# One five-bank score tile for the attention, and the second scan's products in the attention's ring

## The chip, the cores and the metric

The kernel runs on one core of one Trainium2 chip. The metric is the device time of one execution in microseconds (us); the kernel before took 2292.06 us, the median of three runs (2285.45 to 2292.4). Lower is better. TensorE (PE) multiplies matrices, VectorE (DVE) and ScalarE (ACT) work on vectors and read the matmul results out of PSUM, GpSimd (POOL) works on SBUF alone, SyncE (SP) issues the DMAs. PSUM has eight banks here, each 128 partitions by 512 float32 columns. "Granted clock" is the share of its full 2.4 GHz that TensorE ran at.

## The reference

Two layers run over 1280 tokens (256 of context, then 1024 latent ones). In each, one normalised input goes through one input projection into three parallel branches whose outputs are joined by one output projection:

```python
def hybrid_layer(x_l, x_c, mod_l, mod_c, ...):
    h_l = rmsnorm(x_l) * (1 + scale_l) + shift_l          # the same for the context
    p_l = split_cols(h_l @ w_in, IN_SPLITS)
    gdn_c, gdn_l = gdn_branch(...)    # gated DeltaNet: 4 heads, chunks of 64, a scan both ways
    mla_c, mla_l = mla_branch(...)    # 8 heads of softmax attention
    gla_c, gla_l = gla_branch(...)    # gated linear attention: 4 heads, a scan both ways
    x_l = x_l + gate_l * (jnp.concatenate([gdn_l, mla_l, gla_l], axis=-1) @ w_out)

def attend(q, k, v):
    s = jnp.einsum('bqhd,bkhd->bhqk', q, k).astype(jnp.float32) * MLA_SCALE
    p = jax.nn.softmax(s, axis=-1).astype(v.dtype)
    return jnp.einsum('bhqk,bkhd->bqhd', p, v)
```

Latent queries attend to all 1280 keys, context queries to the 256 context keys. In the last layer the context's outputs are not needed and are left out.

## The kernel before, in words

A layer runs in stages (`run`, L1432): the input projection and the preparation of the scans, `up` (the attention's query, key and value projections), `attend` (L1147), `proj_start` (L1309: it loads and transposes the branches' outputs, splits the first weights of the output projection and makes the gates), and `proj`. Beside `up` and `attend` a *background* generator is drawn forward, one step at each `yield` of the attention: the DeltaNet scan `gdn_scan` (20 steps; its first product on TensorE is `kS`, L743), `gla_prep`, eight levels `gla_level` of GLA (score products `gsc`, L887 and L906, then copies into `A`, then new operands `qx` and `kc`, L937, and the decays, L919), and `gla_scan` (10 steps: a transpose `kdt`, outputs `gO`, the state's update `gF`). What of it is left after `attend` is drained there.

The attention's unit is 128 queries of one head: 64 units in layer 1, and in layer 0 the same 64 and eight context units of two tiles each. For a wide unit `first` forms 1024 score columns (tile `sa`: 2 buffers of two banks) and their row maximum (L1219); `second` forms the last 256 (`sb`, half a bank for each of two units), their maximum (L1238), joins both (L1239), and takes two exponentials into `P` (L1240, L1241), each with its row sum. A product by split halves (`mm3`, L254) is three matmuls (L256 to L258). `transposed` turns `P` in groups of 4, 4 and 2 blocks (`ptr`, L1256) and copies them to `PT` (L1260: ACT, DVE, ACT). After each four units `output` multiplies by the values (`O`, L1268).

PSUM in this stage: `sa` 4 banks, `sb` 1, ring "t" 2 (`ptr` and `O` take turns in it), "l" 1 (all that the background's GLA and `proj_start` put in PSUM). Program order is the order of emission in Python, in which the background's last step comes within the first dozen or so units. A scheduler then fixes a static order on each engine, and every engine works through its own in that order; buffers of one ring are still given out in the order of emission.

Of the kernel before, what the change touches and what calls it, by code (L numbers as in the profile page):

```python
# [9 lines left out]
F32 = mybir.dt.float32  # L10
F32R = mybir.dt.float32r
U32 = mybir.dt.uint32
AF = mybir.ActivationFunctionType
ALU = mybir.AluOpType
AX = mybir.AxisListType
# [4 lines left out]
T = 1280  # L20
CT = 2
# [23 lines left out]
class Net:  # L45
# [893 lines left out]
    def gla_scan(self, l):  # L939
        nc, sp = self.nc, self.sp  # L940
        last = l == L - 1
        mm = nc.tensor.matmul
        V, A, P = nc.vector, nc.scalar, nc.gpsimd
        Q, K, tot = (self.lst[n] for n in ("Q", "K", "tots"))

        def at(i):

            return self.A5[i // 2][:, 512 * (i % 2):512 * (i % 2) + 512]

        oL = [self.bp.tile([128, 512], F32, name="oL", tag="oL", bufs=5) for _ in range(5)]  # L950
        order = (tuple(range(10)), (1, 0) + tuple(range(9, 1, -1)))
        S = [None, None]
        for st in range(10):
            vs, kt = [], None
            for d in range(2):
                vv = sp.tile([128, 256], F32, name="gvt", tag="gvt", bufs=4)
                nc.sync.dma_start(vv, self.gv_d[l][order[d][st]])
                vs.append(vv)
            if st < 9:
                pk = self.g("kdt", "l")  # L960
                for d in range(2):
                    i = order[d][st]
                    nc.tensor.transpose(pk[:, 128 * d:128 * d + 128], K[d][:, 128 * i:128 * i + 128], self.ident)
                kt = sp.tile([128, 256], F32, name="ktl", tag="ktl", bufs=2)
                A.copy(kt, pk[:, 0:256])
                yield
            todo = [d for d in range(2) if not (last and order[d][st] < CT) and (d == 0 or S[d] is not None)]
            if todo:
                ps = self.g("gO", "l")
                for d in todo:  # L970
                    i = order[d][st]
                    pd = ps[:, 256 * d:256 * d + 256]
                    if S[d] is not None:
                        mm(pd, Q[d][:, 128 * i:128 * i + 128], S[d], start=True, stop=(d == 1))
                    if d == 0:
                        for hd in range(4):
                            mm(pd[:, 64 * hd:64 * hd + 64], at(i)[:, 128 * hd:128 * hd + 128], vs[0][:, 64 * hd:64 * hd + 64],
                               start=(S[d] is None), stop=(S[d] is None or hd == 3))
                for d in todo:
                    i = order[d][st]  # L980
                    o = oL[i // 2][:, 256 * (i % 2):256 * (i % 2) + 256]
                    pd = ps[:, 256 * d:256 * d + 256]

                    other = (1 - i if i < 2 else 11 - i) if d == 0 else i
                    if st < other or (d == 0 and i == 1):
                        A.copy(o, pd)
                    else:
                        V.tensor_tensor(o, pd, o, ALU.add)
                yield
            if st < 9:  # L990
                pf = self.g("gF", "l")
                for d in range(2):
                    mm(pf[:, 256 * d:256 * d + 256], kt[:, 128 * d:128 * d + 128], vs[d], start=True, stop=True)
                Sn = sp.tile([128, 512], F32, name="Sl", tag="Sl", bufs=2)
                V.tensor_tensor(Sn.rearrange("p (d n) -> p d n", d=2), pf.rearrange("p (d n) -> p d n", d=2),
                                self.bdm.unsqueeze(1).broadcast_to([128, 2, 256]), ALU.mult)
                for d in range(2):
                    Sd = Sn[:, 256 * d:256 * d + 256]
                    if S[d] is not None:
                        i = order[d][st]  # L1000
                        V.scalar_tensor_tensor(Sd, S[d], tot[:, d, i:i + 1], Sd, ALU.mult, ALU.add)
                    S[d] = Sd
            for j in {1: (0,), 7: (2, 3), 9: (1, 4)}.get(st, ()):
                self.head_norm(l, 1, oL[j], j)
            yield
# [141 lines left out]
    def attend(self, l, fill=None):  # L1147
        nc, sp = self.nc, self.ap
# [34 lines left out]

        groups = [(m, i) for m in range(4) for i in range(lt0, NT, 2)]
        units = [(m, i + j, hh) for m, i in groups for hh in range(2) for j in range(1 if i < CT else 2)]
        sb, mxs, sas, ps, PT, rds = {}, {}, {}, {}, {}, {}

        def scores(u, dst, c0, cn, j=0):
            m, i, hh = units[u]
            q, k = [t[:, hh] for t in qTs[m, i - i % 2][0:2]], kTs[m][hh]  # L1190
            J = slice(128 * (i % 2 + j), 128 * (i % 2 + j) + 128)
            self.mm3(dst, q[0][:, J], q[1][:, J], k[0][:, c0:c0 + cn], k[1][:, c0:c0 + cn], True, True)
# [7 lines left out]
                if (m, i - i % 2) not in qTs:  # L1200
                    load_q(m, i - i % 2)

        def first(u, c0):

            m, i, hh = units[u]
            if i < CT:
                if c0 == 0:
                    sas[u] = sa = self.ps.tile([128, 1024], F32, name="sa", tag="sa", bufs=2)[:, 0:512]
                    for j in range(2):
                        scores(u, sa[:, 256 * j:256 * j + 256], 0, 256, j)  # L1210
                    mxs[u] = mx = sp.tile([128, 2], F32, name="mx", tag="mx", bufs=4)
                    V.tensor_reduce(mx, sa.rearrange("p (j k) -> p j k", j=2), AX.X, ALU.max, negate=True)
                return
            if c0 == 0:
                sas[u] = self.ps.tile([128, 1024], F32, name="sa", tag="sa", bufs=2)
            scores(u, sas[u][:, c0:c0 + 512], c0, 512)
            if c0 == 512:
                mxs[u] = mx = sp.tile([128, 2], F32, name="mx", tag="mx", bufs=4)
                V.tensor_reduce(mx[:, 0:1], sas[u], AX.X, ALU.max, negate=True)  # L1219

        def second(u):

            m, i, hh = units[u]
            mx, ta = mxs.pop(u), sas.pop(u)
            if hh == 0 and i % 2 == 0:
                rds[m, i] = sp.tile([128, 2, 2, 2], F32, name="rd", tag="rd", bufs=3)
            r = rds[m, i - i % 2][:, hh, i % 2, :]
            ps[u] = p = self.ab.tile([128, T], F32, name="P", tag="P", bufs=PB)
            if i < CT:
                for j in range(2):  # L1230
                    J = slice(256 * j, 256 * j + 256)
                    A.activation(p[:, J], ta[:, J], AF.Exp, bias=mx[:, j:j + 1], accum_out=r[:, j:j + 1])
                return
            if u // 2 not in sb:
                sb[u // 2] = self.ps.tile([128, 512], F32, name="sb", tag="sb", bufs=1)
            tb = sb[u // 2][:, 256 * (u % 2):256 * (u % 2) + 256]
            scores(u, tb, 1024, 256)
            V.tensor_reduce(mx[:, 1:2], tb, AX.X, ALU.max, negate=True)  # L1238
            V.tensor_tensor(mx[:, 0:1], mx[:, 0:1], mx[:, 1:2], ALU.min)  # L1239
            A.activation(p[:, 1024:T], tb, AF.Exp, bias=mx[:, 0:1], accum_out=r[:, 1:2])  # L1240
            A.activation(p[:, 0:1024], ta, AF.Exp, bias=mx[:, 0:1], accum_out=r[:, 0:1])  # L1241

        def transposed(u, ka):
            m, i, hh = units[u]
# [18 lines left out]
        def output(m, i):  # L1263
# [4 lines left out]
                    mm(po[64 * h2:64 * h2 + 64, 0:256], vv[m][:, 128 * k + 64 * h2:128 * k + 64 * h2 + 64],  # L1268
                       PT[h2][:, k, :], start=(k == 0), stop=(k == nk - 1))
            ri = sp.tile([128, 2, 2], F32, name="ri", tag="ri", bufs=2)  # L1270
            if i < CT:
                V.reciprocal(ri, rd[:, :, 0, :])
            else:
                V.tensor_tensor(ri, rd[:, :, :, 0], rd[:, :, :, 1], ALU.add)
                V.reciprocal(ri, ri)
            for h2 in range(2):
                dg = sp.tile([128, 256], F32, name="dg", tag="dg", bufs=2)
                for x in range(2):
# [7 lines left out]

        n = len(units)
        prepare(0)
        first(0, 0)
        first(0, 512)  # L1290
        for u in range(n + 1):
            if u + 1 < n:
                prepare(u + 1)
            if u < n:
                second(u)
                yield
            for x in range(3):
                if u > 0:
                    transposed(u - 1, 4 * x)
                    yield  # L1300
                if u + 1 < n and x < 2:
                    first(u + 1, 512 * x)
                    yield
            if u > 0 and (u == n or units[u][0:2] not in (units[u - 1][0:2], (units[u - 1][0], units[u - 1][1] + 1 - 2 * (units[u - 1][1] % 2)))):
                output(units[u - 1][0], units[u - 1][1] - units[u - 1][1] % 2)
                yield
# [294 lines left out]
```

## Time and profile before

| | |
|---|---|
| median of three runs | 2292.06 us (2285.45 to 2292.4) |
| the profiled execution | 2287.46 us, span 2285.8 us, mean granted clock 0.945 |
| busy, share of the span | PE 90%, PEld 75%, DVE 56%, ACT 41%, POOL 33% |
| attention of layer 0 | 635 to 1075 us: 440 us, PE busy 406.56 |
| attention of layer 1 | 1757 to 2154 us: 397 us, PE busy 370.83 |
| from there to the end, layer 1 | 2154 to 2286 us, PE busy 101.77 of 132 |

The span is the profiler's; the profiled execution took 1.66 us more, outside it. Busy time is the sum over an engine's instructions without overlaps. The mean over the span hides the stages: TensorE waits little within the attention, and more between the stages.

### The profile page before, as it was taken

The numbers are of one execution on the slowest core, as the hardware profiler recorded it, in microseconds if no ns is written. First come the engines' busy times: TensorE is split into PE (matmuls) and PEld (weight loads), VectorE is DVE, ScalarE is ACT, GpSimd is POOL, SyncE is SP. The second block draws the span as 40 slices with busy tenths as digits, with TensorE's granted clock in tenths as the row PEclk, the third lists the DMA queues.
The fourth block names the chain that finished last, engine by engine and source line by source line (L and its number), as shares of the span: only waits on it lengthen the run. The fifth ranks groups of instructions, "written<-read, shape, count | busy, mean of one in ns | idle before, by whom it ended". The sixth has DMA issues, their size and how long they took to land.

```text
span 2285.8 us, 44471 instructions
## 1 busy us (share of the span) xinstructions
PE 2047.4 (90%) x17820; PEld 1714.2 (75%) x17820; DVE 1279.5 (56%) x2187; ACT 944.3 (41%) x1926; POOL 748.7 (33%) x936
## 2 busy tenths in 40 slices
PE   5998998899989988898997998997897999889688
PEld 3987896777767756676996987896786776667488
DVE  3456466423447689656326355676234667975434
ACT  3346321434235466545204355221642446564421
POOL 1333247122334543214103322374123345420410
PEclk7999999799989999999997999998997999999889
DMA  7111343269642231113524111344355233111433
GB/s 297 46 63 61 101 128 99 71 205 306 206 104 78 72 115 36 40 47 116 172 91 170 62 49 60 106 119 123 118 185 151 58 99 120 32 36 33 138 107 107
DMA packets 207550, 247.33 MB, mean 108 GB/s; under 512 B 60976, under 2 KB 164464, under 8 KB 203760
## 3 DMA queue, kind: packets, MB, share of 16 engines
q1 hardware_dynamic: 207344, 244.49, 34.3%
q8 instruction: 140, 2.29, 0.4%
q14 instruction: 66, 0.54, 0.1%
HBM read 168.14 MB, written 76.28 MB: 107 GB/s over the span
## 4 chain that ended last, share of the span: by engine, by line
PE 62%; DVE 12%; DMA 9%; ACT 6%; POOL 5%; issue 5%; SPq 1%; DVEq 0%; POOLq 0%; ACTq 0%
PE O L1268 6%; PE ptr L1256 4%; PE ptk L256 4%; PE ptk L257 4%; PE ptk L258 4%; PE po L256 3%; PE po L257 3%; PE po L258 3%; PE sa L256 2%; DVE acc L346 2%; PE sa L257 2%; PE sa L258 2%; PE pin L257 2%; PE pin L258 2%; PE pin L256 2%
## 5 line engine op out<-in xcount | busy, mean ns | idle before, releaser
L256 PE MATMUL ptk<-whi,hhi 128*128 128x256 f32 (+1 forms) x912 | 268.7, 295 | 21.1 <-ACT ev L298 12.3
L258 PE MATMUL ptk<-whi,hlo 128*128 128x256 f32 (+1 forms) x912 | 265.8, 293 | 1.6 <-issue 1.1
L257 PE MATMUL ptk<-wlo,hhi 128*128 128x256 f32 (+1 forms) x912 | 266.5, 293 | 0.4 <-DVE wlo L251 0.4
L1256 PE MATMUL ptr<-c_id,P 128*128 128x128 f32 x1312 | 203.5, 283 | 23.0 <-ACT PT L1260 9.7
L1260 ACT COPY PT<-ptr 128x512 f32<-128x512 f32 (+1 forms) x256 | 122.8, 481 | 222.0 <-PE ptr L1256 220.3
L256 PE MATMUL pin<-hhi,whi 128*128 128x512 f32 (+1 forms) x544 | 199.9, 368 | 8.1 <-DVE ev L421 6.8
L1256 PEld LDWEIGHTS ptr<-c_id,P 128*128 128x128 f32 x1312 | 150.4, 142 | 72.7 <-ACT PT L1260 20.8
L256 PEld LDWEIGHTS ptk<-whi,hhi 128*128 128x128 f32 x912 | 184.0, 202 | 26.0 <-ACT ev L298 12.7
L258 PE MATMUL pin<-hhi,wlo 128*128 128x512 f32 (+1 forms) x544 | 198.9, 366 | 0.0
L257 PE MATMUL pin<-hlo,whi 128*128 128x512 f32 (+1 forms) x544 | 198.0, 364 | 0.0
L1219 DVE TENSOR_REDUCE mx<-sa 128x1 f32<-128x1024 f32 x128 | 156.3, 1221 | 60.8 <-PE sa L258 60.2
L258 PEld LDWEIGHTS ptk<-whi,hlo 128*128 128x128 f32 x912 | 183.3, 202 | 4.7 <-issue 3.5
L257 PEld LDWEIGHTS ptk<-wlo,hhi 128*128 128x128 f32 x912 | 184.1, 202 | 2.5 <-issue 1.5
L256 PE MATMUL po<-wohi,yh 128*128 128x256 f32 x576 | 165.2, 287 | 15.3 <-ACT yh L1365 14.1
L1268 PE MATMUL O<-PT,vv 128*64 128x256 f32 x1312 | 169.9, 387 | 1.0 <-ACT PT L1260 0.9
L257 PE MATMUL po<-wolo,yh 128*128 128x256 f32 x576 | 164.3, 286 | 0.0
L258 PE MATMUL po<-wohi,yl 128*128 128x256 f32 x576 | 162.0, 285 | 0.0
L251 POOL TENSOR_TENSOR wlo<-wst,whi 128x1024 fp32r<-128x1024 f32 x32 | 84.0, 2638 | 195.6 <-ACT whi L250 195.6
L1241 ACT ACTIVATE P<-sa,mx 128x1024 f32<-128x1024 f32 x128 | 142.4, 1112 | 0.0
L1268 PEld LDWEIGHTS O<-PT,vv 128*64 128x64 f32 x1312 | 97.0, 138 | 57.7 <-issue 11.4
L256 PE MATMUL sa<-kTh,qTh 128*128 128x512 f32 (+1 forms) x272 | 118.7, 437 | 22.1 <-ACT kTh L1165 16.1
L256 PEld LDWEIGHTS po<-wohi,yh 128*128 128x128 f32 x576 | 111.7, 194 | 16.3 <-ACT yh L1365 14.8
(340 smaller groups left out, 5019.3 us busy)
## 6 DMA issues: line engine op xcount, KB each, us to landing
wada<-in_w_ada_dram SPq DMA_DIRECT2D x24, 1024.0 KB
wst<-in_w_in_dram SPq DMA_DIRECT2D x48, 512.0 KB
kv<-ktv_d SPq DMA_DIRECT2D x80, 128.0 KB
wost<-in_w_out_dram SPq DMA_DIRECT2D x16, 512.0 KB
xt<-in_x_all_dram SPq DMA_DIRECT2D x10, 512.0 KB
at_d<-D SPq DMA_DIRECT2D x4, 1280.0 KB
kn_d<-uo SPq DMA_DIRECT2D x20, 256.0 KB
v_d<-uo SPq DMA_DIRECT2D x20, 256.0 KB
```

The costliest lines, as they stand in the source:

```text
L251: E.tensor_tensor(lo[:, h], st, hi[:, h].bitcast(F32), ALU.subtract)
L256: mm(out, lh, rh, start=first, stop=False)
L257: mm(out, lh, rl, start=False, stop=False)
L258: self.last_mm = mm(out, ll, rh, start=False, stop=last)
L346: nc.vector.scalar_tensor_tensor(a, raw[:, tap:tap + 1282], cw[:, ti, tap:tap + 1], a, ALU.mult, ALU.add)
L1219: V.tensor_reduce(mx[:, 0:1], sas[u], AX.X, ALU.max, negate=True)
L1241: A.activation(p[:, 0:1024], ta, AF.Exp, bias=mx[:, 0:1], accum_out=r[:, 0:1])
L1256: nc.tensor.transpose(tp[:, 128 * (k - ka):128 * (k - ka) + 128], p[:, 128 * c:128 * c + 128], self.ident)
L1260: (V.tensor_copy if ka == 4 else A.copy)(PT[hh][:, ka:kb, 128 * (i % 2):128 * (i % 2) + 128], tp[:, 0:128 * (kb - ka)].rearrange("p (k t) ...
L1268: mm(po[64 * h2:64 * h2 + 64, 0:256], vv[m][:, 128 * k + 64 * h2:128 * k + 64 * h2 + 64], PT[h2][:, k, :], start=(k == 0), stop=(k == nk - 1))
```

## The change

Scores: one tile `sc` of five banks (2560 columns) takes the place of `sa` and `sb`. Unit u writes the 1280 columns of half u % 2; the middle bank, columns 1024 to 1535, holds the end of the even units' half and the start of the odd units'. `first` is now three pieces, cut at the banks; one maximum over 1280 columns (L1227) and one exponential over 1280 (L1242) follow, and the joining of maxima (L1239) and of sums (L1274) goes. The attention yields seven times a unit, where it yielded six times.

GLA scan: `kdt` uses the two halves of one "l" tile in turn, and `gO` and `gF` are taken from ring "t", which `ptr` and `O` use too.

```diff
+        W = self.g("kdt", "l")
         for st in range(10):
...
-                pk = self.g("kdt", "l")
+                pk = W[:, 256 * (st % 2):256 * (st % 2) + 256]
...
-                ps = self.g("gO", "l")
+                ps = self.g("gO", "t")
...
-                pf = self.g("gF", "l")
+                pf = self.g("gF", "t")
...
-        sb, mxs, sas, ps, PT, rds = {}, {}, {}, {}, {}, {}
+        mxs, ps, PT, rds = {}, {}, {}, {}
+        both = self.ps.tile([128, 2 * T], F32, name="sc", tag="sc", bufs=1)
+
+        def room(u):
+
+            return both[:, T * (u % 2):T * (u % 2) + T]
+
+        def pieces(u):
+            return (((0, 512), (512, 512), (1024, 256)), ((0, 256), (256, 512), (768, 512)))[u % 2]
...
-            if c0 == 0:
-                sas[u] = self.ps.tile([128, 1024], F32, name="sa", tag="sa", bufs=2)
-            scores(u, sas[u][:, c0:c0 + 512], c0, 512)
-            if c0 == 512:
+            c0, cn = pieces(u)[x]
+            scores(u, S[:, c0:c0 + cn], c0, cn)
+            if x == 2:
                 mxs[u] = mx = sp.tile([128, 2], F32, name="mx", tag="mx", bufs=4)
-                V.tensor_reduce(mx[:, 0:1], sas[u], AX.X, ALU.max, negate=True)
+                V.tensor_reduce(mx[:, 0:1], S, AX.X, ALU.max, negate=True)
...
-            if u // 2 not in sb:
-                sb[u // 2] = self.ps.tile([128, 512], F32, name="sb", tag="sb", bufs=1)
-            tb = sb[u // 2][:, 256 * (u % 2):256 * (u % 2) + 256]
-            scores(u, tb, 1024, 256)
-            V.tensor_reduce(mx[:, 1:2], tb, AX.X, ALU.max, negate=True)
-            V.tensor_tensor(mx[:, 0:1], mx[:, 0:1], mx[:, 1:2], ALU.min)
-            A.activation(p[:, 1024:T], tb, AF.Exp, bias=mx[:, 0:1], accum_out=r[:, 1:2])
-            A.activation(p[:, 0:1024], ta, AF.Exp, bias=mx[:, 0:1], accum_out=r[:, 0:1])
+            A.activation(p, S, AF.Exp, bias=mx[:, 0:1], accum_out=r[:, i % 2:i % 2 + 1])
```

The first place is TensorE in layer 0, where GLA's score products begin. Before, they stand between the transposes (`ptr`) and score products (`sb`, `sa`) of the attention, at its 264th `ptr` of 672:

```order
L887 MATMUL gsc<-qx_7352,KK 32x128 [waits DMAHW4_49,Activation_49,Pool_49]
L887 MATMUL gsc<-qx_7352,KK 32x128 x15
L1256 MATMUL ptr<-c_id,P 128x128 [waits DVE_49]
L1256 MATMUL ptr<-c_id,P 128x128
L1256 MATMUL ptr<-c_id,P 128x128 [waits Activation_49]
L1256 MATMUL ptr<-c_id,P 128x128 x3
L887 MATMUL gsc<-qx_7353,KK 32x128 [waits DVE_49,Pool_49]
L887 MATMUL gsc<-qx_7353,KK 32x128 x15
```

Now they follow the last DeltaNet step (`kS`, `Tr`, `F`) at the 66th `ptr` of 672, and follow one another:

```order
L753 MATMUL Tr<-r,TT 64x64 [waits DVE_49,PE_49]
L753 MATMUL Tr<-r,TT 64x64 x7
L772 MATMUL F<-vn,at 64x64 [waits DMAHW7_49,DVE_49]
L772 MATMUL F<-vn,at 64x64 [waits DMAHW0_49]
L772 MATMUL F<-vn,at 64x64 x6
L887 MATMUL gsc<-qx_7309,KK 32x128 [waits DVE_49,DMAHW6_49,Activation_49,Pool_49]
L887 MATMUL gsc<-qx_7309,KK 32x128 x15
L887 MATMUL gsc<-qx_7310,KK 32x128 [waits DVE_49,Activation_49,Pool_49]
L887 MATMUL gsc<-qx_7310,KK 32x128 x15
L887 MATMUL gsc<-qx_7309,KK 32x128 [waits DVE_49,Activation_49]
```

From the 66th `ptr` on, six DeltaNet steps and then all 26 rounds of `gsc` stand on TensorE without one instruction of the attention between them; after them `kdt`, `gO` and `gF` alternate with `ptr` 66 to 98, and from the 98th the attention is alone. In layer 1 it is seven steps, all of `gsc` at the 68th `ptr` of 640, and the GLA scan up to the 104th. The gates and the transposes of `proj_start` (`gate`, `ytr`) stand behind the attention before, and within it now.

The second place is TensorE in the attention. Before, a unit's last 256 score columns (`sb`) and the next unit's first 1024 (`sa`) wait for ScalarE apart, with transposes between them:

```order
L256 MATMUL sb<-kTh,qTh 128x256 [waits Activation_49]
L257 MATMUL sb<-kTl,qTh 128x256
L258 MATMUL sb<-kTh,qTl 128x256
L1256 MATMUL ptr<-c_id,P 128x128 [waits DVE_49]
L1256 MATMUL ptr<-c_id,P 128x128 x3
L256 MATMUL sa<-kTh,qTh 128x512 [waits Activation_49]
L257 MATMUL sa<-kTl,qTh 128x512
L258 MATMUL sa<-kTh,qTl 128x512
```

Now the nine score products of an even unit stand together behind one wait, then ten transposes, then the next (odd) unit's:

```order
L256 MATMUL sc<-kTh,qTh 128x512 [waits Activation_49]
L257 MATMUL sc<-kTl,qTh 128x512
L258 MATMUL sc<-kTh,qTl 128x512
L256 MATMUL sc<-kTh,qTh 128x512
L257 MATMUL sc<-kTl,qTh 128x512
L258 MATMUL sc<-kTh,qTl 128x512
L256 MATMUL sc<-kTh,qTh 128x256
L257 MATMUL sc<-kTl,qTh 128x256
L258 MATMUL sc<-kTh,qTl 128x256
L1257 MATMUL ptr<-c_id,P 128x128 [waits PE_49]
L1257 MATMUL ptr<-c_id,P 128x128 x3
```

The wait at the head of each unit's score products is for the exponential of the unit just before, for even and for odd units; before, `sa` waited for the exponential of the unit two before. Once in four units the products by the values stand ahead of such a wait, 13 to 17 of their 20 rows (each is two matmuls in the trace).

## Rows read from the trace of the kernel before

**Rows 1.** Windows: busy of PE, PEld, DVE, ACT, POOL, then granted clock, DMA

```profile
635.00:1075.00 440.00, 406.56 (x3673) 303.35 (x3675) 312.97 (x598) 239.39 (x562) 166.22 (x214) 0.96 0.25 71
800.00:900.00 100.00, 84.48 (x917) 59.91 (x915) 88.98 (x148) 61.65 (x138) 45.10 (x54) 0.93 0.27 81
1757.00:2154.00 397.00, 370.83 (x3416) 280.34 (x3417) 278.89 (x538) 214.03 (x490) 144.09 (x180) 0.98 0.22 64
1905.76:1926.34 20.58, 19.44 (x155) 14.40 (x154) 15.94 (x29) 12.58 (x28) 16.45 (x17) 1.00 0.29 76
2160.00:2185.00 25.00, 8.37 (x36) 7.71 (x37) 3.74 (x4) 8.85 (x12) 15.98 (x10) 0.50 0.79 256
```

**Rows 2.** Waits of PE in 635 to 1075: us in total, times, longest

```profile
PE sb L256 <- ACT P L1240: 6.9, 4, 2.7
```

**Rows 3.** Timeline of PE, layer 1: start us, us, instruction, [idle before <-releaser]

```profile
1915.22 0.51 PE L256 MATMUL sa<-kTh,qTh 128*128 128x512 f32 x1 [0.48 <-ACT P L1241]
...
1916.49 0.39 PE L258 MATMUL sa<-kTh,qTl 128*128 128x512 f32 x1
1916.72 1.59 PE L1256 MATMUL ptr<-c_id,P 128*128 128x128 f32 x10
1918.12 0.39 PE L256 MATMUL sb<-kTh,qTh 128*128 128x256 f32 x1
...
1921.03 4.54 PE L1268 MATMUL O<-PT,vv 128*64 128x256 f32 x40
```

**Rows 4.** Timeline of ACT at the same place

```profile
1913.16 0.37 ACT L1260 COPY PT<-ptr 128x256 f32<-128x256 f32 x1 [0.94 <-PE ptr L1256]
...
1913.97 1.11 ACT L1241 ACTIVATE P<-sa,mx 128x1024 f32<-128x1024 f32 x1
```

**Rows 5.** Groups by form, whole span: busy us, mean ns, idle before

```profile
L1219 DVE TENSOR_REDUCE mx<-sa 128x1 f32<-128x1024 f32 x128 | 156.3, 1221 | 60.8 <-PE sa L258 60.2
L1241 ACT ACTIVATE P<-sa,mx 128x1024 f32<-128x1024 f32 x128 | 142.4, 1112 | 0.0
L1240 ACT ACTIVATE P<-sb,mx 128x256 f32<-128x256 f32 x128 | 61.2, 478 | 46.1 <-DVE mx L1239 45.1
L1238 DVE TENSOR_REDUCE mx<-sb 128x1 f32<-128x256 f32 x128 | 53.4, 417 | 10.6 <-PE sb L258 7.4 <-ACT PT L1260 0.5
```

**Rows 6.** Timeline of PE in layer 0: DeltaNet's steps, then GLA's first products

```profile
615.97 1.15 PE L743 MATMUL kS<-Sg,KQ 64*64 64x64 f32 x32
622.61 1.65 PE L743 MATMUL kS<-Sg,KQ 64*64 64x64 f32 x26 [0.52 <-DVE oS L775]
...
639.94 1.97 PE L743 MATMUL kS<-Sg,KQ 64*64 64x64 f32 x32
...
774.35 1.15 PE L743 MATMUL kS<-Sg,KQ 64*64 64x64 f32 x32
...
807.71 1.08 PE L887 MATMUL gsc<-qx,KK 128*32 128x128 f32 x32 [0.65 <-DMA KK<-gqk_d]
```

**Rows 7.** Groups of DVE in 800 to 960: busy us, mean ns

```profile
L937 DVE COPY qx<-QQ 32x512 f32<-32x512 f32 (+1 forms) x46 | 20.3, 441 | 1.4 <-PE gsc L887 0.3
L919 DVE TENSOR_TENSOR KK<-KK,al 128x640 f32<-128x640 f32 x14 | 17.2, 1258 | 0.1
L919 DVE TENSOR_TENSOR QQ<-QQ,al 128x640 f32<-128x640 f32 x14 | 14.6, 1083 | 0.0
L892 DVE COPY_PREDICATED A<-c_gmask,gsc 128x512 f32<-128x512 uint32 (+1 forms) x15 | 9.4, 628 | 0.2
```

**Rows 8.** Timeline of PE in layer 1: a step of the GLA scan

```profile
2120.45 1.00 PE L977 MATMUL gO<-gvt,A 128*128 128x64 f32 x8
...
2123.11 1.03 PE L993 MATMUL gF<-gvt,ktl 128*128 128x256 f32 x4
```

**Rows 9.** Waits of PE in 2154 to 2192

```profile
PE po L256 <- ACT yh L1365: 14.1, 2, 12.7
PE ytr L1363 <- DMA yx<-y_d: 5.5, 1, 5.5
```

More of the change, by code (lines that the diff above doesn't have):

```diff
@@ L964, in gla_scan @@
                 kt = sp.tile([128, 256], F32, name="ktl", tag="ktl", bufs=2)
-                A.copy(kt, pk[:, 0:256])
+                A.copy(kt, pk)
                 yield
@@ L1201, in prepare, with first @@
                     load_q(m, i - i % 2)
-        def first(u, c0):
+        def first(u, x):
             m, i, hh = units[u]
+            S = room(u)
             if i < CT:
-                if c0 == 0:
-                    sas[u] = sa = self.ps.tile([128, 1024], F32, name="sa", tag="sa", bufs=2)[:, 0:512]
+                if x == 0:
                     for j in range(2):
-                        scores(u, sa[:, 256 * j:256 * j + 256], 0, 256, j)
+                        scores(u, S[:, 256 * j:256 * j + 256], 0, 256, j)
                     mxs[u] = mx = sp.tile([128, 2], F32, name="mx", tag="mx", bufs=4)
-                    V.tensor_reduce(mx, sa.rearrange("p (j k) -> p j k", j=2), AX.X, ALU.max, negate=True)
+                    V.tensor_reduce(mx, S[:, 0:512].rearrange("p (j k) -> p j k", j=2), AX.X, ALU.max, negate=True)
                 return
-            if c0 == 0:
-                sas[u] = self.ps.tile([128, 1024], F32, name="sa", tag="sa", bufs=2)
-            scores(u, sas[u][:, c0:c0 + 512], c0, 512)
-            if c0 == 512:
+            c0, cn = pieces(u)[x]
+            scores(u, S[:, c0:c0 + cn], c0, cn)
+            if x == 2:
                 mxs[u] = mx = sp.tile([128, 2], F32, name="mx", tag="mx", bufs=4)
-                V.tensor_reduce(mx[:, 0:1], sas[u], AX.X, ALU.max, negate=True)
+                V.tensor_reduce(mx[:, 0:1], S, AX.X, ALU.max, negate=True)
         def second(u):
             m, i, hh = units[u]
-            mx, ta = mxs.pop(u), sas.pop(u)
+            mx, S = mxs.pop(u), room(u)
             if hh == 0 and i % 2 == 0:
-                rds[m, i] = sp.tile([128, 2, 2, 2], F32, name="rd", tag="rd", bufs=3)
-            r = rds[m, i - i % 2][:, hh, i % 2, :]
+                rds[m, i] = sp.tile([128, 2, 2], F32, name="rd", tag="rd", bufs=3)
+            r = rds[m, i - i % 2][:, hh]
             ps[u] = p = self.ab.tile([128, T], F32, name="P", tag="P", bufs=PB)
@@ L1231, in second @@
                     J = slice(256 * j, 256 * j + 256)
-                    A.activation(p[:, J], ta[:, J], AF.Exp, bias=mx[:, j:j + 1], accum_out=r[:, j:j + 1])
+                    A.activation(p[:, J], S[:, J], AF.Exp, bias=mx[:, j:j + 1], accum_out=r[:, j:j + 1])
                 return
-            if u // 2 not in sb:
-                sb[u // 2] = self.ps.tile([128, 512], F32, name="sb", tag="sb", bufs=1)
-            tb = sb[u // 2][:, 256 * (u % 2):256 * (u % 2) + 256]
-            scores(u, tb, 1024, 256)
-            V.tensor_reduce(mx[:, 1:2], tb, AX.X, ALU.max, negate=True)
-            V.tensor_tensor(mx[:, 0:1], mx[:, 0:1], mx[:, 1:2], ALU.min)
-            A.activation(p[:, 1024:T], tb, AF.Exp, bias=mx[:, 0:1], accum_out=r[:, 1:2])
-            A.activation(p[:, 0:1024], ta, AF.Exp, bias=mx[:, 0:1], accum_out=r[:, 0:1])
+            A.activation(p, S, AF.Exp, bias=mx[:, 0:1], accum_out=r[:, i % 2:i % 2 + 1])
         def transposed(u, ka):
@@ L1270, in output @@
             ri = sp.tile([128, 2, 2], F32, name="ri", tag="ri", bufs=2)
[L1271 to L1275, printed above, removed]
+            V.reciprocal(ri, rd)
             for h2 in range(2):
@@ L1288, in attend @@
         prepare(0)
-        first(0, 0)
-        first(0, 512)
+        for x in range(3):
+            first(0, x)
         for u in range(n + 1):
@@ L1300, in attend @@
                     yield
-                if u + 1 < n and x < 2:
-                    first(u + 1, 512 * x)
+                if u + 1 < n:
+                    first(u + 1, x)
                     yield
```

## The prediction

> **What bounds the kernel now.** I read the windows by stage first, then TensorE's waits, then its timeline, and last the background's groups and ScalarE's timeline. The two attention stages take 440 and 397 us, with TensorE busy 92% and 93% of them [rows 1]: it is the limit there, with the background's products filled in between those of the attention. In layer 0 its longest wait on the softmax, of `sb` for the exponential, is 6.9 us in all [rows 2]. Where almost nothing but the attention runs, in layer 1, four units take 20.58 us at the full clock, 19.44 of it busy [rows 1]; taking off 1.2 us for two DeltaNet products in that stretch (an estimate, half of a `kS` of 1.15 each [rows 6]) leaves 4.85 us a unit. The timeline shows its content: six score products in 1.66 us (1915.22 to 1916.88), three more of 256 columns in about 0.5, ten transposes in 1.4 to the next product (1916.72 to 1918.12), and 4.5 us of products by the values each fourth unit [rows 3]. So a change that only lightens VectorE and ScalarE gains little, and a new wait of TensorE costs its full length.
>
> **The new order of the background.** Buffers of ring "t" are given out as emitted. The GLA scan is emitted within the first units, and its `gO` and `gF` now take turns with `ptr` in that ring. Every later `ptr` has to come behind the scan, and the scan behind DeltaNet and all eight levels. The order shows just that: the attention stops at `ptr` 66 of 672 (68 of 640 in layer 1). Before, this chain had the whole stage for it. I price it piece by piece, layer 0 first.
>
> *Up to the stop*: 11 `kS` stand beside the attention before, 13.4 us apart (639.94 to 774.35 [rows 6]). Six are alone now, so five remain beside it: 67 at that pace at most, and at least 51 by the units (six wide ones at the pace below, two context ones at half of it, and 8 for the first loads). I take 57.
>
> *DeltaNet alone*: two steps just ahead of the attention stand 6.64 us apart (615.97, 622.61), which is the chain through VectorE and GpSimd with little beside it. The last `kS` to the first `gsc` takes 33.4 [rows 6]. Five gaps and that tail are 66.6; I take 67, and 73 in layer 1, with seven steps.
>
> *The levels alone*: before they go from 807.71 to about 959, 151 us, beside the attention, with VectorE busy 88.98 of 100 [rows 1, 6]. Their own VectorE work in that stretch is at least 20.3 + 17.2 + 14.6 + 9.4 = 61.5 us [rows 7]. A round, however, is a chain: `gsc` 1.08, the copy out 0.63 and a hop, with the single "l" bank between two rounds, so about 1.9; 26 rounds, seven of them half size, make some 43, and L919 of each level, which the next level waits for, adds 31.8 as measured. That is 75. TensorE is then busy about half the time. In the stretch 2160 to 2185 it is busy a third, and the granted clock is 0.50 [rows 1]; at that level each full `gsc` takes another 1.08, and the rounds, worth 22.5 full ones, add 24: 99. I take 84, and 72 in layer 1, which has eight tiles of the ten.
>
> *The GLA scan with 3.2 units*: one step from `gO` to the end of `gF` took 3.7 (2120.45 to 2124.14 [rows 8]) with little in between; ten steps less one, and 3.2 units at 6.2, are 53 to 57. I take 55 and 53.
>
> **The new score chain.** What follows is the attention alone, for some 57 units of layer 0 (55 wide, and the rest of the context) and 53.6 of layer 1. Each unit's products now wait for the exponential of the unit before. The maximum over 1280 is the line through 417 ns at 256 and 1221 at 1024: 1.49 us; the exponential likewise from 478 and 1112: 1.32 [rows 5]. From the start of the exponential over 1024 to the product that it releases were 1.25 (1913.97 to 1915.22 [rows 3, 4]), so 1.46 for 1280. The circle is 2.2 (nine products and the pipeline's end) + 1.49 + 1.46 + two hops of 0.05 = 5.25 us. The ten transposes fit under the maximum and the exponential (2.95). The last eviction of `PT`, 0.37 [rows 4], stands on ScalarE ahead of the exponential and pushes it by about 0.25: 5.5. Once in four units 13 to 17 of the 20 rows by the values stand before the next products: 2.9 to 3.8 us of the 4.54 [rows 3] plus 1.4 of transposes, against a cover of 2.95, so 1.3 to 2.3 more, 0.3 to 0.6 a unit. With the casts of queries and keys on ScalarE (an estimate: 0.2 a unit) it is 6.0 to 6.4; I take 6.2. TensorE would then be busy 4.85 of 6.2, 78%, somewhat below the 84% of the stretch 800 to 900, where the clock was 0.93 [rows 1].
>
> The operations that go are worth 0.25 of maximum and join and 0.46 of exponential a unit; both engines leave gaps in the steady part, so I count them at nothing beyond the circle, which contains them.
>
> **Behind the attention.** `ytr`, the gates and the first weights are moved into it. In layer 1 TensorE waits there 14.1 + 5.5 us, and 25 us pass at half the clock [rows 1, 9]. The last tiles still have to come. Bounds 0 and 20 in layer 1, 0 and 5 in layer 0; I take 16 in all.
>
> **The sum.** Layer 0: 57 + 67 + 84 + 55 + 57 x 6.2 (353) = 616 against 440, +176. Layer 1: 50 + 73 + 72 + 53 + 53.6 x 6.2 (332) = 580 against 397, +183. With -16: +343. The profiled execution took 2287.5, so 2630; the median of the runs lies 4.6 higher, so **2635 us**.
>
> **Rivals.**
> *The score wait costs nothing*: if even units in effect start while the exponential runs, the attention stays at 4.85 a unit, and only the stall is paid. 57 x 4.85 = 276 makes layer 0 540 (+100), 53.6 x 4.85 = 260 makes layer 1 508 (+111), with -16 +195: 2485. For it: an even unit's first 1024 columns lie in two banks that the odd unit before doesn't touch. Against it: the order puts the wait at the first piece of every unit. The Trainium skill ("PSUM — Partial Sum Buffer", section "PSUM bank collisions raise a hardware error") wants guards by bank and quadrant, not by address: by that, two of the three pieces of an even unit need no wait, the circle of that unit would be about 1.5 us shorter, and this rival's time would follow; no row here shows a bank that two units share.
>
> *The clock falls in the pauses*: at half the clock the nine products take 2.2 more and a fourth unit's block 4.5 more; half of the 110 units so, at some 2.2 each, are +120: 2750. For it: the 0.50 of 2160 to 2185; against: 84% busy kept 0.93 [rows 1].
>
> *The levels keep their pace of before* (151 instead of 84, in layer 1 less): +120, also 2750. Against it: VectorE's 89 of 100 were mostly the attention's.
>
> *Not slower*: both stalls vanish because the stage is bound by TensorE's work, not by the order. Then 34 and 26 us of TensorE's idle time in the two stages [rows 1] come back in part, and 16 behind them: 2240 to 2290. It decides if a unit's circle stays under 4.85 and the attention runs beside the levels. The first is missed by 0.4 at the least that I can make of the rows; the second is excluded by an order in which no row of the attention stands between the levels.
>
> **How the numbers follow.** The forecast 0.63, with its own range 2560 to 2700. The score wait that costs nothing 0.12, the clock 0.12, the levels 0.05, not slower 0.04, other mishaps 0.04. The low end reaches into the first rival from 2490, the high end half way to the two at 2750: range 2490 to 2725. A measurement of this kernel can tell about 0.3%, 7 us, from no change: slower 0.96, same 0.01, faster 0.03.
>
> **What would show it.** In the profile after: a stretch of about 150 us in each layer with `kS`, then `gsc`, and no `sc`, `ptr` or `O`, TensorE busy half or less. Then waits of `sc` on ScalarE's `P` (L1242) as the largest wait of TensorE, about 1.2 us a unit and 130 to 150 in all; starts of the maximum 6.0 to 6.4 us apart; 1.49 for it and 1.32 for the exponential. `po` waiting little for `yh`. It is wrong if `sc` stands beside `gsc` in time, if the steady unit takes under 5.5 us, or if attention's stages take less than 520 us.

## The result: 17% slower

The changed kernel took 2686.14 us (median of four runs, 2683.28 to 2688.8) against 2290.68 for the kernel before on the same chip: a ratio of 1.1731, 95% interval 1.1706 to 1.1755, or 395 us more. Forecast were 2635 us and 2490 to 2725: right in direction, in range, and 51 us short.

Each layer's attention is counted from the start of its first score product to the start of its last `ym`, the operation of 0.42 us that ends it. So cut, the profiled executions divide like this (us; "between" is from the end of layer 0's attention to the start of layer 1's, "behind" from the end of layer 1's attention to the end of the span; what is left of the span lies ahead of layer 0's attention):

| kernel | attention 0 | between | attention 1 | behind | span |
|---|---|---|---|---|---|
| before | 445.5 | 667.7 | 406.1 | 131.5 | 2285.8 |
| after | 662.2 | 665.0 | 620.9 | 100.5 | 2687.0 |

So all of the loss lies in the two attention stages, +217 and +215, and 31 us come back behind layer 1.

### The profile page after: what moved, and what is told of

The parts are those of the page before. It is cut to its first block, busy times and chain, and to the rows that moved or that the text cites. A ratio compares the mean times of both kernels' runs of the same rounds, so it can differ in the third digit from the quotient of the medians.

```text
span 2687.0 us, 44032 instructions
## 1 busy us (share of the span) xinstructions
PE 2179.8 (81%) x17820; PEld 1800.4 (67%) x17820; DVE 1243.3 (46%) x1899; ACT 920.5 (34%) x1670; POOL 741.5 (28%) x936
## 5 line engine op out<-in xcount | busy, mean ns | idle before, releaser
L1227 DVE TENSOR_REDUCE mx<-sc 128x1 f32<-128x1280 f32 x128 | 190.8, 1491 | 355.5 <-PE sc L258 355.5
L256 PE MATMUL sc<-kTh,qTh 128*128 128x512 f32 (+1 forms) x400 | 175.4, 438 | 110.6 <-ACT P L1242 92.3
L1257 PE MATMUL ptr<-c_id,P 128*128 128x128 f32 x1312 | 212.7, 296 | 39.7 <-ACT PT L1261 32.7
L1257 PEld LDWEIGHTS ptr<-c_id,P 128*128 128x128 f32 x1312 | 161.8, 152 | 89.4 <-ACT PT L1261 57.5
L256 PEld LDWEIGHTS sc<-kTh,qTh 128*128 128x128 f32 x400 | 85.3, 213 | 153.8 <-ACT P L1242 112.6
L1242 ACT ACTIVATE P<-sc,mx 128x1280 f32<-128x1280 f32 x128 | 170.4, 1332 | 48.8 <-DVE mx L1227 48.2
L257 PE MATMUL sc<-kTl,qTh 128*128 128x512 f32 (+1 forms) x400 | 160.1, 400 | 1.3 <-POOL kTl L1167 1.3
L258 PE MATMUL sc<-kTh,qTl 128*128 128x512 f32 (+1 forms) x400 | 160.2, 400 | 0.0
```

What stands on the lines that cost most here:

```text
L256: mm(out, lh, rh, start=first, stop=False)
L257: mm(out, lh, rl, start=False, stop=False)
L258: self.last_mm = mm(out, ll, rh, start=False, stop=last)
L1227: V.tensor_reduce(mx[:, 0:1], S, AX.X, ALU.max, negate=True)
L1242: A.activation(p, S, AF.Exp, bias=mx[:, 0:1], accum_out=r[:, i % 2:i % 2 + 1])
L1257: nc.tensor.transpose(tp[:, 128 * (k - ka):128 * (k - ka) + 128], p[:, 128 * c:128 * c + 128], self.ident)
```

## The profile after

The windows of the changed kernel, cut where the prediction cut them: in layer 0 the attention up to the stop, DeltaNet alone, the levels alone, the GLA scan, the attention alone; then the same five of layer 1, and what lies behind. Columns as in [rows 1].

```profile
638.00:707.00 69.00, 57.54 (x628) 44.38 (x630) 31.66 (x54) 22.65 (x42) 24.54 (x35) 0.88 0.31 82
707.00:774.00 67.00, 29.41 (x474) 25.42 (x470) 20.20 (x48) 4.78 (x8) 33.06 (x38) 0.54 0.23 72
774.00:866.00 92.00, 45.60 (x608) 31.03 (x608) 66.28 (x121) 36.75 (x79) 27.45 (x40) 0.52 0.06 22
866.00:924.00 58.00, 51.20 (x277) 40.03 (x278) 27.77 (x50) 17.24 (x38) 10.85 (x11) 0.88 0.18 55
924.00:1301.00 377.00, 299.42 (x1741) 214.82 (x1740) 146.85 (x192) 155.46 (x285) 77.76 (x99) 0.91 0.17 48
1965.00:2026.00 61.00, 51.31 (x558) 39.73 (x560) 30.76 (x47) 21.38 (x35) 20.44 (x28) 0.92 0.30 81
2026.00:2104.00 78.00, 35.27 (x560) 30.53 (x558) 23.70 (x55) 6.34 (x11) 34.61 (x40) 0.54 0.23 74
2104.00:2182.00 78.00, 34.98 (x480) 24.59 (x480) 57.49 (x94) 26.72 (x54) 26.29 (x33) 0.50 0.05 17
2182.00:2236.00 54.00, 46.71 (x262) 35.41 (x263) 25.98 (x48) 17.26 (x37) 8.39 (x9) 0.92 0.21 64
2236.00:2587.00 351.00, 278.33 (x1653) 200.58 (x1652) 138.07 (x171) 143.20 (x248) 68.60 (x82) 0.92 0.16 48
2587.00:2687.00 100.00, 90.75 (x761) 90.33 (x760) 40.72 (x69) 17.35 (x38) 7.90 (x10) 0.98 0.35 121
```

Read the first number after the window, its length, and the second, TensorE's busy time. From 707 to 866 TensorE is busy under half the time, and the granted clock is at or near its lower level. From 924 on only the attention is left, with a few gates and transposes of `proj_start`, and still a fifth of the time is idle. No product of the attention starts between 704.4 and 869.6 in layer 0, and between 2025.2 and 2186.0 in layer 1. TensorE's timeline at the stop shows two steps of DeltaNet that follow one another, and where GLA begins:

```profile
707.80 1.15 PE L743 MATMUL kS<-Sg,KQ 64*64 64x64 f32 x32 [0.52 <-DVE oS L775]
710.40 0.68 PE L753 MATMUL Tr<-r,TT 64*64 64x64 f32 x16 [1.45 <-DVE r L746]
711.65 0.68 PE L761 MATMUL F<-vn,kv 64*64 64x64 f32 x16 [0.56 <-issue]
712.91 1.12 PE L772 MATMUL F<-vn,at 64*64 64x64 f32 x16 [0.58 <-DVE Sg L767]
714.55 1.97 PE L743 MATMUL kS<-Sg,KQ 64*64 64x64 f32 x32 [0.52 <-DVE oS L775]
717.80 1.12 PE L753 MATMUL Tr<-r,TT 64*64 64x64 f32 x16 [1.28 <-DVE r L746]
719.49 1.12 PE L761 MATMUL F<-vn,kv 64*64 64x64 f32 x16 [0.56 <-issue]
721.19 1.12 PE L772 MATMUL F<-vn,at 64*64 64x64 f32 x16 [0.58 <-DVE Sg L767]
722.83 1.97 PE L743 MATMUL kS<-Sg,KQ 64*64 64x64 f32 x32 [0.52 <-DVE oS L775]
...
774.37 1.94 PE L887 MATMUL gsc<-qx,KK 128*32 128x128 f32 x32 [17.59 <-ACT qx L878]
```

The first of the two takes 6.75 us, close to the 6.64 of [rows 6], at a granted clock of 0.87; the second takes 8.28, at 0.50. Its four groups of products take 5.33 us where they took 3.63: that covers the difference. The five steps alone in layer 0 are 6.8, 8.3, 11.5, 8.2 and 8.3 us apart; the 11.5 was not taken apart. `gsc` takes 1.94 us where it took 1.08 in [rows 6].

TensorE's timeline in the attention alone, first products of four units in a row and the block by the values between the second and the third:

```profile
1234.23 0.38 PE L256 MATMUL sc<-kTh,qTh 128*128 128x256 f32 x1 [1.08 <-ACT P L1242]
...
1239.63 0.50 PE L256 MATMUL sc<-kTh,qTh 128*128 128x512 f32 x1 [1.78 <-ACT P L1242]
...
1243.67 4.10 PE L1269 MATMUL O<-PT,vv 128*64 128x256 f32 x34 [0.46 <-ACT PT L1261]
1247.70 0.38 PE L256 MATMUL sc<-kTh,qTh 128*128 128x256 f32 x1
...
1253.80 0.50 PE L256 MATMUL sc<-kTh,qTh 128*128 128x512 f32 x1 [0.45 <-ACT P L1242]
```

The steps are 5.40, 8.07 and 6.10 us; the circle, the circle behind a block by the values, and the circle again. The product at 1239.63 belongs to an even unit (its first piece is 512 wide), and its wait ends with the exponential of the odd unit before. VectorE and ScalarE between those two products:

```profile
1236.35 1.49 DVE L1227 TENSOR_REDUCE mx<-sc 128x1 f32<-128x1280 f32 x1 [3.02 <-PE sc L258]
```

```profile
1237.89 0.37 ACT L1261 COPY PT<-ptr 128x256 f32<-128x256 f32 x1 [0.53 <-PE ptr L1257]
1238.16 1.33 ACT L1242 ACTIVATE P<-sc,mx 128x1280 f32<-128x1280 f32 x1
```

Products from 1234.23, maximum from 1236.35 to 1237.84, the copy of the last transposes in between, exponential from 1238.16, next products at 1239.63: nothing of the circle overlaps with itself. The Trainium skill ("PSUM — Partial Sum Buffer", section "PSUM bank collisions raise a hardware error") asks for guards by bank and quadrant; by that the even unit's first two pieces, in banks that the odd unit doesn't use, need none. The trace shows the wait of 1.78 us all the same. It is no single case: in both layers each of the 134 units behind a first one starts its products at least 0.14 us after the end of the exponential of the unit just before, 83 of them within 0.2. That the framework keeps the dependency for the whole tile is my reading of this; no kernel was built to show it. No run here shows two engines in a shared bank: no score product overlaps a read of its tile, neither in `sc` nor in `sb` of the kernel before, whose bank two units share.

The waits of TensorE in 924 to 1301 (us in total, times, longest), beside which the 6.9 of [rows 2] stand, and then the one wait listed behind layer 1 (2587 to 2630), which answers to [rows 9]:

```profile
PE sc L256 <- ACT P L1242: 48.1, 37, 2.8
PE ptr L1257 <- ACT PT L1261: 15.5, 35, 1.2
```

```profile
PE po L256 <- ACT wohi L250: 1.2, 1, 1.2
```

The groups of the two merged operations, answering to [rows 5]:

```profile
L1227 DVE TENSOR_REDUCE mx<-sc 128x1 f32<-128x1280 f32 x128 | 190.8, 1491 | 355.5 <-PE sc L258 355.5
L1242 ACT ACTIVATE P<-sc,mx 128x1280 f32<-128x1280 f32 x128 | 170.4, 1332 | 48.8 <-DVE mx L1227 48.2
```

1.491 and 1.332 us are what the lines through [rows 5] gave, to 0.01. VectorE now idles 355 us ahead of the maximum, for products that wait for the exponential.

## The experiments

The ten kernels, with their stages (as in the table above):

| kernel | median us | ratio (95%) | attention 0 | between | attention 1 | behind |
|---|---|---|---|---|---|---|
| scores_only | 2333.06 | 1.0164 (1.0128 to 1.0200) | 479.8 | 665.8 | 445.1 | 99.5 |
| scan_only | 2484.59 | 1.0824 (1.0784 to 1.0864) | 557.3 | 668.0 | 524.1 | 100.9 |
| after_slow_draw | 2385.23 | 1.0407 (1.0379 to 1.0434) | 476.3 | 689.2 | 445.7 | 131.9 |
| scan_every4th | 2357.21 | 1.0279 (1.0252 to 1.0307) | 489.2 | 665.0 | 456.8 | 99.0 |
| after_max_twice | 2903.68 | 1.2684 (1.2656 to 1.2712) | 773.1 | 665.8 | 719.8 | 101.1 |
| before_max_twice | 2362.36 | 1.0314 (1.0284 to 1.0344) | 470.4 | 681.1 | 434.6 | 132.7 |
| after_evict_dve | 2657.43 | 1.1611 (1.1580 to 1.1642) | 639.7 | 661.4 | 613.1 | 99.9 |
| scan_late_then_fast | 2299.93 | 1.0051 (1.0032 to 1.0070) | 456.6 | 665.2 | 436.4 | 99.9 |
| layer1_scan_3rd2nd | 2291.23 | 1.0007 (0.9986 to 1.0027) | 445.2 | 678.3 | 423.0 | 104.4 |
| layer1_scan_2nd1st | 2293.08 | 1.0017 (1.0002 to 1.0032) | 448.4 | 677.1 | 426.2 | 99.6 |

### The two parts apart

**scores_only**: the change with the old `gla_scan`.

```diff
-                ps = self.g("gO", "t")
+                ps = self.g("gO", "l")
...
-                pf = self.g("gF", "t")
+                pf = self.g("gF", "l")
```

(and `kdt` from "l" at each step again). 

> The score part alone: the five-bank tile with one maximum and one exponential a unit, and the GLA scan with its products in the bank of its own as before. Theory (the new circle of products, maximum and exponential has gaps of TensorE, and the background fills them while it lasts; the long stretch in which the attention was alone is what made them cost): 2280 to 2360 us, most likely 2310, attention stages of 430 to 480 and 400 to 440 us. Rival (the circle costs its 6.2 to 6.6 us a unit whatever stands beside it, and adds to the background's own time): half or more of the whole loss stays, 2470 to 2520. Second rival (the circle is hidden entirely and the operations saved count): under 2275.

Measured: +41 us. The theory holds, though layer 1's 445.1 lies above the 400 to 440 that it gave, and the circle is not hidden entirely. With the background beside it, it costs 34 and 39 us in the two attentions, and 32 come back behind layer 1. Its waits in layer 0's attention (643 to 1123):

```profile
PE sc L256 <- ACT P L1241: 19.1, 27, 4.1
```

(L1241 is the one exponential there.) 19.1 us for all of the stage, where the changed kernel has 48.1 in its last 377.

**scan_only**: the kernel before with the new `gla_scan` alone. 

> The scan part alone: the second scan's products in the attention's ring, the score tiles as before. Theory (ring order forces the background ahead, and the attention waits for DeltaNet, the levels and the scan one after the other; the attention alone then runs at TensorE's 4.85 us a unit): a stretch of some 160 us in each layer without attention, 2460 to 2510 us, 2480 most likely. Rival (the stall is the whole loss, and the score circle was covered): 2600 to 2690. Second rival (the stall alone costs little, since TensorE's work is the same): under 2400.

Measured: +192 us, within 5 us of the theory. Its windows of DeltaNet alone, the levels alone, and the attention alone in layer 0:

```profile
708.00:776.00 68.00, 29.76 (x474) 25.72 (x470) 20.34 (x48) 5.21 (x9) 32.97 (x38) 0.54 0.24 75
776.00:869.00 93.00, 45.51 (x609) 31.13 (x610) 65.91 (x121) 36.78 (x78) 27.24 (x40) 0.54 0.06 20
...
924.00:1198.00 274.00, 250.07 (x1687) 184.57 (x1688) 158.44 (x294) 156.58 (x375) 75.88 (x98) 0.98 0.21 61
```

The same stall, to a us or two, with the old score tiles: it is the scan part's alone. (The scan part also changes the tile of `kdt`, and no run moves `gO` and `gF` by themselves; of the three only these two stand in the attention's ring.) And where the changed kernel then needs 377 us from 924 on, this one needs 274 for nearly the same work, 546 `ptr` against 571.

The two parts alone add up to 41 + 192 = 233; together they cost 395. The 162 between are the interaction: the stall takes away the background that filled the circle's gaps, which the next run bears out. The score part is worth 41 us where the background lies beside the attention, and 2686 - 2485 = 201 where the attention is alone.

### The order of emission

**after_slow_draw**: the whole change, drawn more slowly.

```diff
-                for _ in self.attend(l):
-                    if bg is not None and next(bg, bg) is bg:
+                for y, _ in enumerate(self.attend(l)):
+                    if y % 6 == 0 and bg is not None and next(bg, bg) is bg:
```

> The whole change, but the background is drawn forward only at every sixth yield of the attention, so that its scan is emitted late in the attention and the ring's turns come late too. Nothing else is changed. Theory (order of emission in the ring is what starved the attention): the stretch without attention is gone, GLA's levels stand beside the attention again, 2290 to 2380 us, 2330 most likely (no gain behind the attention, since gates and transposes stand behind it). Rival (the five-bank tile makes the attention slow by itself): 2480 to 2600. Second rival (the products in the shared ring hold up the transposes step by step wherever they stand): 2400 to 2480.

Measured: 301 us of the 395 come back with a line that changes no operation and no buffer. The attentions, 476 and 446 us, are those of scores_only: at this pace the shared ring shows no price there (a small one may hide, since scores_only has the gates and transposes in its attentions too). The stall is gone: two neighbouring products of the attention are nowhere more than 8.2 us apart in their starts, where it was 165 and 161. So the theory holds on what starved the attention, but its range, 2290 to 2380, was missed by 5 us and its 2330 by 55. Against scores_only the 52 us more are at the ends. Gates and transposes fall behind the attention again: 131.9 instead of 99.5 behind layer 1, which the theory had counted, and 21 us more than in the kernel before behind layer 0, where the granted clock is 0.64 (1112 to 1160), which it had not. The other part that it lacked is the attentions' 31 and 40 over the kernel before.

### The circle

**after_max_twice** and **before_max_twice**: the line of the large maximum written twice, in the change and in the kernel before.

```diff
                 V.tensor_reduce(mx[:, 0:1], S, AX.X, ALU.max, negate=True)
+                V.tensor_reduce(mx[:, 0:1], S, AX.X, ALU.max, negate=True)
```

> The whole change, with the maximum over 1280 taken twice for every wide unit (the same result written again), 1.49 us more on VectorE each time. Theory (products, maximum and exponential of a unit are one circle, and the attention alone goes round it): the 111 units that run alone each take up to 1.49 us more, less where the products by the values already stand in the way once in four: 110 to 165 us more, 2790 to 2850. Rival (TensorE's own work, at the lower clock, sets the pace of 6.6 us a unit, and the wait for the exponential only shows it): under 30 more.

> The kernel before, with the maximum over 1024 taken twice, 1.22 us more on VectorE for each of 128 wide units, 156 in all. Theory (with two score tiles the maximum is off the circle, and only the stretch of the levels, where VectorE is 89% busy, feels it, some 25 units in each layer at most): 2295 to 2340. Rival (maximum and exponential are as much on the path here as after the change): 2400 or more.

Measured: +217.5 on the change, 1.70 us for each of 128 wide units, and +73 on the kernel before, 0.57. The first is above the theory's 110 to 165, and its 2790 to 2850 was missed; the rival, under 30, is far off. All 128 units at 1.49 would make 191; that those at the products by the values paid in full is not shown. The rest goes with a lower clock, 0.82 in layer 0's attention alone against 0.91. VectorE and TensorE in one such unit:

```profile
1256.04 1.49 DVE L1227 TENSOR_REDUCE mx<-sc 128x1 f32<-128x1280 f32 x1 [4.49 <-PE sc L258]
1257.57 1.49 DVE L1228 TENSOR_REDUCE mx<-sc 128x1 f32<-128x1280 f32 x1
```

```profile
1252.53 0.39 PE L256 MATMUL sc<-kTh,qTh 128*128 128x256 f32 x1 [2.55 <-ACT P L1243]
...
1253.25 0.63 PE L257 MATMUL sc<-kTl,qTh 128*128 128x512 f32 x1
...
1260.63 0.58 PE L256 MATMUL sc<-kTh,qTh 128*128 128x256 f32 x1 [2.68 <-ACT P L1243]
```

8.10 us from unit to unit, with VectorE idle for 4.49 before the first maximum. That is 2.70 more than the 5.40 of the changed kernel: 1.53 for the second maximum, and 1.39 because the products take 3.51 us to the maximum instead of 2.12 (a product 512 wide takes 0.63 here and 0.39 there), less what the other steps give back. In the kernel before I had the price too low: 2295 to 2340 expected, 2362 measured (and 2400 or more by the rival). Of the 73, 25 and 28 lie in the two attentions, 13 between them and 8 ahead of the first; the first score product starts anywhere from 634 to 644 us in the kernels here, so the 8 say little, and the 13 were not taken apart. With two tiles a maximum costs a third to a half of its time (53 or 73 of 156), not nothing.

**after_evict_dve**: a copy of 0.37 us taken from ahead of the exponential.

```diff
-                (V.tensor_copy if ka == 4 else A.copy)(
+                (A.copy if ka == 0 else V.tensor_copy)(
```

> The whole change, with the copy of the last two transposes (0.37 us on ScalarE, ahead of the exponential) given to VectorE. Theory (that copy pushes the exponential by 0.25 us and is part of the circle): 111 units at 0.2 to 0.27 less: 20 to 30 us less, 2655 to 2670. Rival (the copy fits in the pause before the maximum is done): no change, 2680 to 2692.

Measured: 29 us less than the change (2657.43; 2686.14), as the theory said: 0.26 for each of the 111 units that run alone. It is not spread evenly: layer 0's attention is 22.5 us shorter and layer 1's 7.8, and why was not looked into. The waits for the exponential in the attention alone of layer 0 (930 to 1270) fell from 48.1 to 31.0:

```profile
PE sc L256 <- ACT P L1242: 31.0, 27, 2.4
```

### Versions that might have won

Every kernel whose gates and transposes stand within layer 1's attention saved some 30 us behind it. Four kernels took the old score tiles with the new scan and drew the background by count. **scan_every4th** has `y % 4` in the line shown above; the others draw at `y % self.every`, and set it anew where `gla_scan` begins: 5 and then 3 in **scan_late_then_fast**; 6, and then 3 in layer 0 and 2 in layer 1, in **layer1_scan_3rd2nd**; 6, and then 3 and 1, in **layer1_scan_2nd1st**.

> The score tiles as before, the scan part of the change, and the background drawn forward at every fourth yield, so that the scan is spread over the middle of the attention and ends before it does; the gates and layer 1's transposes then stand within the attention. Theory (no stall, TensorE bound at its old pace, and the 20 to 30 us behind layer 1's attention saved): 2250 to 2285 us, 2268 most likely. Rival (products in the shared ring cost transposes their turn): 2300 to 2350. Second rival (the background's end is not what the stage behind waits for): 2285 to 2300.

> The score tiles as before and the scan part of the change; the background is drawn at every fifth yield until the GLA scan begins and at every third from there, so that the levels stand spread over the attention and the scan ends some 100 transposes ahead of its end. Theory (what cost the draw at every fourth yield its gain was the levels bunched in one place, 40 us at half the clock; with them spread, the attention keeps its pace and the stage behind saves 25 to 30 us): 2255 to 2290. Rival (each product of the scan in the shared ring costs the transposes a turn, wherever it stands): 2310 to 2350.

> The score tiles as before, the scan part of the change, the background drawn at every sixth yield (as in the kernel before), and from the GLA scan on at every third in layer 0 and every second in layer 1. Layer 1's transposes behind the scan then begin at its 600th transpose of 640, layer 0 stays as before. Theory (the draw at every fifth yield cost 30 us in layer 1's attention, by levels that again ran into the ring's turns and stood alone for some 20 us at a lowered clock; at every sixth they don't): layer 1's attention 406 to 420 us, 15 to 30 saved behind it: 2265 to 2285. Rival (the work moved into the attention and the shared ring cost what the stage behind saves): 2288 to 2310.

> As the run beside it, but from the GLA scan on the background is drawn at every yield in layer 1, so that the scan takes some 40 transposes of the attention and layer 1's transposes behind it begin at the 560th of 640. Theory: all of the 25 to 30 us behind layer 1 saved, but a scan so dense holds up the attention for its chain, 10 steps of 4 to 5 us against 4 units of 4.85: 10 to 20 lost there; 2270 to 2290. Rival (the dense scan stops the attention as in the whole change): 2300 to 2330.

None of them beat the kernel before: +65, +10, and twice no difference of use (1.0007, 0.9986 to 1.0027, and 1.0017, 1.0002 to 1.0032). All four lie above the range of their theory; only layer1_scan_3rd2nd falls into that of its rival. At every fourth yield a good part of the levels still stood in one block: the attention stops for 42 us in layer 0 and 46 in layer 1, with 192 of the 600 and of the 480 `gsc` in between, and in scan_late_then_fast for 17 in layer 1. The window of scan_every4th 880 to 920, and that of scan_late_then_fast in layer 1, 2002 to 2042:

```profile
880.00:920.00 40.00, 18.65 (x189) 12.39 (x182) 23.64 (x54) 18.10 (x45) 6.96 (x13) 0.50 0.00 1
```

```profile
2002.00:2042.00 40.00, 26.34 (x142) 16.68 (x141) 24.00 (x50) 18.66 (x46) 5.59 (x12) 0.76 0.06 18
```

With the levels at the old pace (the last two) layer 0 is at 445 and 448, as before, but layer 1's attention is 17 and 20 longer and the stage between 9 to 11, against 27 to 32 saved behind: I had expected a net gain, 2265 to 2285 and 2270 to 2290, and the work moved cost at its new place what it saved at the old one. How much of the 17 to 20 is TensorE's time for the moved products and how much the shared ring was not taken apart, nor was the stage between.

## Why the prediction was right, point by point

- *The attention stops and the background runs alone.* Right. DeltaNet alone 67 us (67 forecast) and 78 (73); the levels 92 (84) and 78 (72), near the end of the bounds that was worked out at half the clock, and half the clock it was (0.52, 0.50); the scan 58 (55) and 54 (53). The four groups that I added up for VectorE were 61.5 us [rows 7]; all of it is busy 66.28 there. That DeltaNet alone came out so well is luck: its five steps took 43 us and not 33 (I priced them at the full clock, and one of them is the 11.5), and the way from the last `kS` (750.8) to `gsc` (774.4) took 23.6 and not 33.4 (I took that from a stretch beside the attention). Layer 1 is alike, 52 for 40 and 25 for 33.
- *Up to the stop.* Mis-sized: 69 from the first product against 57, and 61 in layer 1 against 50. The bound by DeltaNet's pace, 67, was the better one: the five `kS` beside the attention stand 13.0 us apart (642.8 to 707.8) where I had 13.4. I chose a value between it and the units' 51.
- *The circle.* Right in kind and in its parts: 1.49 and 1.33 us, 5.40 for a unit that nothing disturbs (5.25 to 5.5). Mis-sized in the mean: 377 us for 57 units are 6.6, and 351 for 53.6 are 6.55, against 6.2. The four units shown, with the step of 5.73 ahead of them (1228.50 to 1234.23), take 25.30, 6.3 each. At 0.35 to 0.4 a unit this term is short by 43 us (24 + 19), the largest single error, and it is not the idle time: TensorE is idle 1.36 us a unit in both layers (77.6 and 72.7 us), against the 1.35 of 6.2 less 4.85. It is busy 5.25 and 5.19 us a unit instead of 4.85, 41 us in all. 14 of them are the gates and transposes that came out of the stage behind; the rest was not taken apart, beside a clock of 0.91 and 0.92. The four parts ahead of this term are short by 46 together. Against these stand 15, since the stages before were 445.5 and 406.1 rather than 440 and 397 long, and 14 at the ends (18 more saved there, 3.5 lost by a later start). That leaves 58 on the profiled spans and 51 on the medians; that it is not 89 is in part luck.
- *Behind the attention.* Mis-sized: 31 us saved in layer 1, above its bound of 20, and 3 in layer 0, twice the 16 in all. The wait of `po` is gone, and TensorE is busy 91 of 100 us there. In layer 0 little could be saved: the gates ran beside the end of the attention already in the kernel before (1069.6 to 1080.5), and 36 of the 40 `ytr` still stand at its end or behind it now (from 1300.1 on).
- *The signs.* The stretch without attention, the largest wait of TensorE and the two durations are as named. The wait of `sc` for `P` is smaller, 48.1 us in layer 0's attention alone (0.84 a unit, not 1.2) and 92.3 in the whole span, not 130 to 150; the rest of the idle time stands before other instructions, such as `ptr` with 15.5. The maxima start 6.77 us apart in layer 1's attention alone (51 of them, 2237.7 to 2576.1), not 6.0 to 6.4.
- *The rivals.* "The score wait costs nothing" is out: scan_only, which is that case built, took 2485 (2485 forecast). "The clock falls in the pauses" is true in kind (0.91, and 0.82 with two maxima), and far smaller than its 120: all of TensorE's added busy time is 41. "The levels keep their pace" is out. "Not slower" failed where the text put its point of decision: the circle is above 4.85, and nothing of the attention stands between the levels.
- *What the prediction did not see.* How far the two parts depend on each other. scores_only shows that the circle costs 34 and 39 us in the two attentions while there is other work to put in its gaps, and whole against scan_only that it costs 105 and 97 where there is none. The sum could come out right since the pace of 6.2 was worked out for an attention without that work.

## What to carry to other kernels

A ring of buffers given out in the order of emission is an order of work: putting a late consumer of a side chain in a ring of the main loop makes the main loop wait for all of that chain, and the profile of before can price it stage by stage. One tile with two halves did not act as two buffers here, which a dependency kept by tile would explain; work out the circle of producer, reader and last reader, and compare it with the busy time of the bound engine in a steady stretch. Fewer and larger operations on engines that waited anyway gained nothing here; how much of the 41 us of scores_only is the one tile's and how much the merged operations' was not separated.

## What the runs showed that I had not expected

Where DeltaNet ran alone, with TensorE busy 29.41 of 67 us, the granted clock went from 0.87 in its first step to 0.50 in its second, and the chain itself got slower: 8.28 us a step instead of 6.75, which TensorE's own products, 1.70 longer, cover. In scan_only three of its five steps are 8.2 to 8.3 us too. And the maximum of the kernel before, on whose path the list of waits shows nothing large, costs 0.41 us in the attentions, 0.57 over the span, for 1.22 of added work.
